# Making the top-k masks inside the first attention head pair, and filling that pair twice as densely

## The chip, the cores and the metric

The kernel runs on one core of a Trainium2 chip. The metric is the device time of one execution in microseconds. Times shown are of three runs of the kernel before; the rows are of one profiled execution.

## The reference

A two-layer streaming trunk on 1024 prompt positions and 64 sample positions (with 512 cached ones), all in one call. What matters here is the attention branch of layer 0:

```
rel   = relu(einsum('bqhd,bsd->bqhs', qi, ki))
score = einsum('bqh,bqhs->bqs', wi, rel)              # one score row per query
adm   = (kpos // 64) <= (qpos // 64)
top_val, top_idx = top_k(where(adm, score, -inf), k)  # 256 keys for a prompt row, 144 for a sample row
logits = einsum(q, k[top_idx]) * 64 ** -0.5
o      = softmax(logits) @ v[top_idx]                 # 8 heads, 2 key/value groups
a_out  = o * silu(ga)
```

The kernel gathers nothing. For each row it finds the k-th largest score by a search, and adds a mask (0 or -1e30) to the logits of all keys; equal scores at the threshold are taken in order of position until k is reached. Beside the attention, a gated short convolution and the projections of both layers have to be computed.

## The kernel before, in words

All activations lie transposed, 128 channels by 1088 positions (1024 prompt, 64 sample). A projection tile is 128 output channels; it is three chunks of positions, each 24 accumulated matmuls (8 slices of the contraction, three products of a high and a low part), 72 matmuls in all.

The layer 0 part goes in this order. The indexer's scores of the seven score blocks (six prompt blocks of 128 queries, whose key ranges are 384 to 1024 wide, and the sample's, 576 wide) are put side by side in one tile S of 4800 columns. `topk` (line 487) then searches the threshold T of every row by halving; its passes run on VectorE and ScalarE, while TensorE works at projection tiles. After that, `mask` (line 592) makes a row block's mask: a sign pass on ScalarE (line 601), and on VectorE a count (602), a comparison for equality (603), a running sum over the equal ones in the tile `cum` (604), and three more passes (605 to 607) that leave the mask in the bf16 tile `bias`. All seven are called in one loop (line 877), at the end of the pool of the search.

Then comes the attention, in four head pairs t = 0 to 3 (line 934). A pair makes its query stacks (`pair_stack`, on ScalarE and POOL), goes through the eight query blocks in the order ORDER[t] (0 to 7 in the first pair), and ends with the sample's. In `attend` a block b with n = 128 (b + 1) keys does, for each of its two heads, `softmax`: logits by TensorE in pieces of at most 512 columns, a fused add of the mask with a running minimum on VectorE into S (line 622), the exponential on ScalarE (625), a reciprocal on VectorE (626) and the scaling on POOL (627). Blocks 0 and 1 read a fixed corner tile in place of `bias`. `weighted` transposes the probabilities in groups of two key tiles on TensorE (650), splits them on ScalarE and VectorE (276, 277), and multiplies with the values (658). The two halves are added into q on VectorE (722; 732 for the sample, which closes the pair).

The probabilities are kept in S itself: `slot` hands out columns one after another and starts again at 0 at the end, so block 0 uses the columns 0 to 256, block 1 those to 768, and so on. S holds the scores until the masks have read them.

What the TensorE queue does between attention steps is laid down by hand. After the Q, K, V, convolution and gate tiles done so far, eleven projection tiles are left (ATTN_TILES): three for Q, four GB and four GA. Their matmuls are handed out one by one by a generator, `tiles` (line 919). First 255 are issued ahead of the pairs (BEFORE). Then each call of `pace` draws a number of them: RATE[t] = (r0, r1, r2) is drawn r0 at each logit piece, r1 at the end of each value group, r2 behind each full group of transposes. The generator takes the tiles in order, and a GA tile t is held until head pair t is done:

```python
while kind == GA and self.done <= t:
    yield
```

A step that meets this line issues nothing. What is left after the fourth pair is issued at once (line 945). The order on each engine's queue is then put together by a planner that takes the earliest traced instruction that its own estimate of durations says is ready; `issue_after` adds an edge that keeps an instruction behind a given one on the same engine. Loads all go through SyncE's queue.

Of the kernel before, what the change touches and what calls it, by code (L numbers as in the profile page):

```python
# [2 lines left out]

# [6 lines left out]
F32 = mybir.dt.float32  # L10
F32R = mybir.dt.float32r
BF = mybir.dt.bfloat16
I32 = mybir.dt.int32
AF = mybir.ActivationFunctionType
OP = mybir.AluOpType
PSUM = bass.MemoryType.PSUM

P = 128
D = 1024
KT = D // P  # L20
SEQ = 1024
DEC = 64
PAST = 512
TC = SEQ + 64
# [7 lines left out]
MASK = -1.0e30  # L32
# [40 lines left out]
NSB = len(SBLK)  # L73
# [11 lines left out]
ORDER = [(0, 1, 2, 3, 4, 5, 6, 7)] + [(7, 0, 6, 1, 5, 2, 4, 3)] * 3  # L85


BEFORE = 255
RATE = ((1, 1, 3),) * 4


def cut(n):
# [5 lines left out]
class Trunk:  # L98
# [388 lines left out]
    def topk(self, pool):  # L487
# [4 lines left out]
        V = nc.vector  # L492

        def t(name, w=NSB):
            return pool.tile([P, w], F32, name=name)

        kk = [TOPK_P] * (NSB - 1) + [TOPK_S]
        steps, upper = 23, 7
        self.kneg = kneg = t("kneg")
        lims, lad = t("lims", 4 * NSB).rearrange("p (i j) -> p i j", i=4), t("lad", steps)  # L500
        for j in range(NSB):
            n, k, p = SW[j], kk[j], slice(COL[j], COL[j] + 1)
# [5 lines left out]
            nc.gpsimd.memset(lad[:, s:s + 1], 2.0 ** -(s + 1))  # L508
        tiny = t("tiny")
        nc.gpsimd.memset(tiny, 2.0 ** -126)  # L510
        cv, m, sgn, limx, T, cand, flag = (t(n) for n in ("cv", "m", "sgn", "limx", "T", "cand", "flag"))
        self.T, self.cv, self.sgn = T, cv, sgn
        junks = [self.cum, pool.tile([P, SEQ], BF, name="junk")]


        small = self.bank("av", "small")
# [43 lines left out]
        for i in range(len(exps) + steps):  # L560
            for n, p in enumerate(SPANS):
                count(n, i < len(exps) + upper)
                if i < len(exps):
                    f, nxt = exps[i], (*exps, 1.0)[i + 1]
                    V.tensor_scalar(g[:, p], m[:, p], nxt - nxt / f, nxt / f, op0=OP.mult, op1=OP.add)
                    V.tensor_mul(cand[:, p], cand[:, p], g[:, p])
                    if i == len(exps) - 1:
# [8 lines left out]
                                       op0=OP.add, op1=OP.mult)  # L576
# [12 lines left out]
        V.tensor_mul(T, T, flag)  # L589
        V.tensor_mul(T, T, sgn)  # L590

    def mask(self, pool, j):

        V = self.nc.vector
        n = SW[j]
        sl = self.S[:, SOFF[j]:SOFF[j] + n]
        bi = self.bias[:, SOFF[j]:SOFF[j] + n]
        p = slice(COL[j], COL[j] + 1)
        thr, c = self.T[:, p], self.cv[:, p]
        cum = self.cum[:, 0:n]  # L600
        self.nc.scalar.activation(sl, sl, AF.Copy, scale=self.sgn[:, p])
        V.tensor_scalar(bi, sl, thr, self.kneg[:, p], op0=OP.is_gt, op1=OP.add, accum_out=c)
        V.tensor_scalar(bi, sl, thr, None, op0=OP.is_equal)
        V.tensor_tensor_scan(cum, self.ones.to_broadcast([P, n]), bi, c, OP.mult, OP.add)  # L604
        V.scalar_tensor_tensor(bi, cum, 0.0, bi, op0=OP.is_gt, op1=OP.mult)
        V.scalar_tensor_tensor(bi, sl, thr, bi, op0=OP.is_lt, op1=OP.add)
        V.tensor_scalar(bi, bi, MASK, None, op0=OP.mult)


    def softmax(self, slot, lhs, keys, g, n, bias):  # L610
# [151 lines left out]
    def layer0(self):  # L762
# [4 lines left out]
        def cols(c):  # L767
            return slice(*CHUNKS[c])

        def into(dst, f=AF.Copy):  # L770
            def evac(c, ps):
                nc.scalar.activation(dst[:, cols(c)], ps, f)
            return evac

        def into_z(z):
            def evac(c, ps):
                a, b = CHUNKS[c]
                for d, e in ((a, min(b, SEQ)), (SEQ, b)):
                    if d < e:
                        o = 2 if d < SEQ else 4  # L780
                        nc.scalar.activation(z[:, o + d:o + e], ps[:, d - a:e - a], AF.Copy)
            return evac
# [16 lines left out]
        def do(kind, t, evac):  # L799
            w = take(kind, t)  # L800
            fetch()
            return self.project(w, evac)

        with ExitStack() as es:
# [37 lines left out]
            kv = es.enter_context(self.pool("kv", "right"))  # L842
            self.kp = [kv.tile([P, 2, TC], F32R, name=f"kp{i}") for i in range(2)]
            self.vs = kv.tile([P, 13, 2, P], F32R, name="vs")
            with self.pool("search", "right") as se:
                def pair():
                    return (se.tile([P, TC], F32, tag="gc", name="gc"),
                            se.tile([P, TC + 4], F32, tag="z", name="z"))

                self.cum = se.tile([P, SEQ], BF, name="cum")  # L850
                self.topk(se)
                se.tile([P, 512], F32, tag="tap", name="place", bufs=1)
                kt, vt = pair()
                self.wslots.append((se, 2))
                hist = se.tile([P, 4, 2], F32, name="hist")
                self.load(hist, self.i["hist"])
                self.hist = hist
                self.tail = se.tile([P, 4, 2, 2], F32, name="tail")

                self.tags = ["pj", "pj", "lg", "lg", "lg"]  # L860
                do(Q_, 0, into(self.q[:, 0, :]))
                do(K_, 0, into(kt))
                do(V_, 0, into(vt))
                self.load(self.o["k"], kt)
                self.load(self.o["v"], vt[:, 0:TC])
                self.keys_values(se, kt, vt)
                for c in range(4):
                    if c >= NGZ:
                        do(GZ, c, into(self.bo[:, c, :], AF.Silu))
                    gc, z = pair()  # L870
                    do(GC, c, into(gc))
                    do(XIN, c, into_z(z))
                    self.conv(se, c, gc, z)
                self.wslots.remove((se, 2))
                self.tags = ["pj"]
                self.load(self.o["conv"], self.tail)
                for j in range(NSB):
                    self.mask(se, j)
            with self.pool("attn", "right") as ap:
                self.at = 0  # L880

                ap.tile([P, TC], F32, tag="ga", name="place")
                self.kc = [ap.tile([P, 2, NS], F32R, name=f"kc{i}") for i in range(2)]
                ap.tile([P, 256], F32, tag="ckr", name="place", bufs=1)
                ap.tile([64, 256], F32, tag="avl", name="place", bufs=2)
                ap.tile([P, P], F32R, tag="qs", name="place", bufs=1)
                ap.tile([P, 512], F32R, tag="ptl", name="place", bufs=2)
                ap.tile([P, 512], F32R, tag="pth", name="place", bufs=2)
                for e in range(2):
                    ap.tile([P, TC], F32R, tag=f"qst{e}", name="place")  # L890

                def gate_b(t):
                    def evac(c, ps):
                        nc.vector.tensor_mul(self.bo[:, t, cols(c)], self.bo[:, t, cols(c)], ps)
                    return evac

                ga = []

                def gate_a(t):
                    def evac(c, ps):  # L900
                        if c == 0:
                            ga[:] = [ap.tile([P, TC], F32, tag="ga", name="ga")]
                        g, q = ga[0], self.q[:, t, :]
                        if t == 3:
                            nc.scalar.activation(g[:, cols(c)], ps, AF.Silu)
                            nc.vector.tensor_mul(q[:, cols(c)], q[:, cols(c)], g[:, cols(c)])
                            return

                        nc.scalar.activation(g[:, cols(c)], ps, AF.Copy)
                        if c == NCH - 1:  # L910
                            nc.scalar.activation(g, g, AF.Silu)
                            nc.gpsimd.tensor_mul(q, q, g)
                    return evac

                evacs = {Q_: lambda t: into(self.q[:, t, :]), GB: gate_b, GA: gate_a}
                left = list(ATTN_TILES)
                self.done = 0

                def tiles():
                    while left:  # L920
                        kind, t = left[0]
                        while kind == GA and self.done <= t:
                            yield
                        key, w = ahead.pop(0)
                        assert key == (kind, t)
                        fetch()
                        yield from self.steps(w, evacs[kind](t), n=1)
                        left.pop(0)
                        yield

                self.side = tiles()
                for _ in range(BEFORE):
                    next(self.side)
                for t in range(4):
                    while (Q_, t) in left:
                        next(self.side)
                    self.rate = RATE[t]
                    st = self.pair_stack(ap, t)
                    for b in ORDER[t]:
                        self.attend(ap, st, t, b)  # L940
                    if t == 0:
                        self.sample_keys(ap)
                    self.attend_sample(ap, st, t)
                    self.done = t + 1
                for _ in self.side:
                    pass
                fetch()
# [273 lines left out]
```

## Time and profile before

| what | us |
|---|---|
| median of 3 runs | 1160.54 |
| lowest, highest | 1160.08, 1160.92 |
| the profiled execution's own time | 1162.17 |
| its span | 1160.5 |
| TensorE busy (share of the span) | 1087.5 (94%) |
| VectorE busy | 670.2 (58%) |
| ScalarE busy | 519.3 (45%) |
| POOL busy | 440.1 (38%) |

The span runs from the first to the last instruction of the program; the execution's own time has what lies around it. Busy times are sums over stages with different limits. In the rows PE is TensorE, DVE is VectorE, ACT is ScalarE, POOL is GpSimd, and L604 is line 604.

### The profile page before, as it was taken

The page shows a single profiled execution, that of the slowest core. Times are in us where ns is not written, and L with a number is a line of the kernel's source. Part 1 is how long each engine was busy: PE and PEld are TensorE (multiplying, and loading weights), DVE is VectorE, ACT ScalarE, POOL GpSimd, SP SyncE. Part 2 cuts the span into 40 slices and gives each one's busy share as a digit, 9 for nine tenths or more (in the row PEclk, how much of TensorE's full clock was granted, in tenths as well). Part 3 has the DMA queues.
Part 4 walks back from the last instruction along what each step waited for, and adds up shares of the span by engine and source line. Part 5 has one row for each costly group of instructions (what it writes and reads, how often), then busy time and mean ns, then how long its engine had stood idle before and what let it go on. Part 6 is the DMA issues. An engine that isn't in the chain of part 4 may idle for free.

```text
span 1160.5 us, 18892 instructions
## 1 busy us (share of the span) xinstructions
PE 1087.5 (94%) x7255; PEld 1044.7 (90%) x7255; DVE 670.2 (58%) x1657; ACT 519.3 (45%) x976; POOL 440.1 (38%) x454
## 2 busy tenths in 40 slices
PE   5899999999999449999999899999999999999997
PEld 4789689999999439989899899999999999999996
DVE  4711799998886987767675524521186055247134
ACT  5232586856777246777666313521121211135111
POOL 2634223466548225464431326531143111154222
PEclk9999999999999769999999999999999999999999
DMA  9745511211101000000002410111112111131012
GB/s 361 302 155 191 201 29 55 80 52 38 37 19 54 25 14 19 19 19 20 19 20 82 160 59 31 44 55 37 37 47 91 37 37 36 38 108 38 1 65 91
DMA packets 26074, 81.84 MB, mean 71 GB/s; under 512 B 3072, under 2 KB 9984, under 8 KB 23552
## 3 DMA queue, kind: packets, MB, share of 16 engines
q1 hardware_dynamic: 25984, 80.63, 19.7%
q8 instruction: 57, 0.93, 0.3%
q14 instruction: 33, 0.27, 0.1%
HBM read 74.50 MB, written 6.12 MB: 69 GB/s over the span
## 4 chain that ended last, share of the span: by engine, by line
PE 81%; DVE 7%; ACT 5%; POOL 3%; issue 3%; DMA 1%; SPq 0%; POOLq 0%; DVEq 0%; ACTq 0%
PE pj L247 40%; PE op L247 15%; PE pj L262 9%; PE av L658 3%; PE logit_ps L620 2%; PE p_ps L650 2%; PE ada_ps L153 2%; PE sgu_ps L1036 1%; PE score_ps L427 1%; PE first L318 1%; POOL w_lo L239 1%; POOL hf L329 1%; DVE cum L604 1%; PE score_ps L428 1%; DVE al L277 1%
## 5 line engine op out<-in xcount | busy, mean ns | idle before, releaser
L247 PE MATMUL pj<-ah,w_hi 128*128 128x364 f32 (+1 forms) x984 | 326.0, 331 | 1.0 <-ACT w_hi L238 1.0
L247 PE MATMUL pj<-al,w_hi 128*128 128x364 f32 (+1 forms) x984 | 323.8, 329 | 0.0
L247 PE MATMUL pj<-ah,w_lo 128*128 128x364 f32 (+1 forms) x984 | 323.1, 329 | 0.0
L239 POOL TENSOR_TENSOR w_lo<-w_raw,w_hi 128x1024 fp32r<-128x1024 f32 x63 | 158.0, 2510 | 341.3 <-ACT w_hi L238 336.4
L247 PEld LDWEIGHTS pj<-ah,w_hi 128*128 128x128 f32 x984 | 185.0, 188 | 2.0 <-ACT w_hi L238 1.3
L247 PEld LDWEIGHTS pj<-ah,w_lo 128*128 128x128 f32 x984 | 184.8, 188 | 0.3 <-issue 0.2
L247 PEld LDWEIGHTS pj<-al,w_hi 128*128 128x128 f32 x984 | 185.0, 188 | 0.0
L247 PE MATMUL op<-ah,w_lo 128*128 128x448 f32 (+2 forms) x384 | 126.2, 330 | 3.1 <-POOL w_lo L239 3.1
L247 PE MATMUL op<-al,w_hi 128*128 128x448 f32 (+2 forms) x384 | 126.5, 330 | 0.7 <-DVE al L277 0.6
L247 PE MATMUL op<-ah,w_hi 128*128 128x448 f32 (+2 forms) x384 | 126.9, 330 | 0.0
L238 ACT ACTIVATE w_hi<-w_raw 128x1024 fp32r<-128x1024 f32 x69 | 72.9, 1058 | 111.6 <-PE pj L247 83.2
L528 DVE TENSOR_SCALAR_CACHE_REDUCE cum<-S,cand 128x512 bf16<-128x512 f32 (+5 forms) x142 | 119.0, 838 | 2.0
L262 PE MATMUL pj<-ah,w_hi 128*128 128x364 f32 (+1 forms) x288 | 96.0, 334 | 0.0
L262 PE MATMUL pj<-ah,w_lo 128*128 128x364 f32 (+1 forms) x288 | 95.2, 330 | 0.0
L262 PE MATMUL pj<-al,w_hi 128*128 128x364 f32 (+1 forms) x288 | 95.1, 330 | 0.0
L976 DVE SCALAR_TENSOR_TENSOR x<-op,mod,x 128x192 f32<-128x192 f32 (+2 forms) x64 | 30.5, 497 | 108.2 <-PE op L247 108.2
L555 ACT ACTIVATE junk<-S,cand 128x896 bf16<-128x896 f32 (+2 forms) x78 | 77.7, 996 | 24.4 <-DVE m L558 20.6
L627 POOL TENSOR_SCALAR S<-S,sm 128x384 f32<-128x384 f32 (+8 forms) x68 | 50.8, 753 | 87.1 <-DVE sm L626 72.7
L620 PE MATMUL logit_ps<-kp,qst 128*128 128x384 f32 (+5 forms) x192 | 49.6, 366 | 33.2 <-DVE sm L622 32.6
L247 PEld LDWEIGHTS op<-ah,w_lo 128*128 128x128 f32 x384 | 73.1, 190 | 5.4 <-POOL w_lo L239 3.5
L247 PEld LDWEIGHTS op<-al,w_hi 128*128 128x128 f32 x384 | 73.0, 190 | 3.4 <-DVE al L277 1.4
L247 PEld LDWEIGHTS op<-ah,w_hi 128*128 128x128 f32 x384 | 73.0, 190 | 2.0
(242 smaller groups left out, 1973.9 us busy)
## 6 DMA issues: line engine op xcount, KB each, us to landing
w_raw<-in_w SPq DMA_DIRECT2D x53, 512.0 KB, 3.4
ada<-in_ada_w SPq DMA_DIRECT2D x19, 1024.0 KB, 7.8
w_raw<-in_wo SPq DMA_DIRECT2D x16, 512.0 KB, 3.4
x<-in_x SPq DMA_DIRECT2D x8, 544.0 KB, 6.5
bo<-in_ada_w SPq DMA_DIRECT2D x4, 1024.0 KB, 6.9
x<-in_x SPq DMA_DIRECT2D x1, 1792.0 KB, 10.2
out_y<-x SPq DMA_DIRECT2D x1, 1792.0 KB, 6.6
x<-in_x SPq DMA_DIRECT2D x1, 1536.0 KB, 8.2
```

Source lines behind the costliest of these rows:

```text
L153: nc.tensor.matmul(pt[32 * g:32 * g + 32, 0:P], self.cs[:, kt, :], raw(kt)[:, g * P:(g + 1) * P], start=kt == 0, stop=kt == KT - 1, tile_p ...
L238: nc.scalar.activation(hi, raw, AF.Copy)
L239: (nc.gpsimd if lo_eng == "pool" else nc.vector).tensor_sub(lo, raw, hi)
L247: last = self.nc.tensor.matmul(ps, wt[:, kt, :], at[:, kt, c0:c1], start=n == 0, stop=n == len(mms) - 1)
L262: self.nc.tensor.matmul(ps, wt[:, kt, :], at[:, kt, a:b], start=kt == 0 and i == 0, stop=kt == KT - 1 and i == 2)
L528: V.tensor_scalar(junks[0][:, 0:SW[j]], self.S[:, span(j)], thr, 0.0, op0=OP.is_lt, op1=OP.add, accum_out=col(cv, j))
L555: nc.scalar.activation(junks[1][:, 0:SW[j]], self.S[:, span(j)], AF.Sign, scale=-1.0, bias=col(cand, j), accum_out=col(cv, j))
L620: mm = nc.tensor.matmul(pt[:, 0:w], lhs, keys[i][:, g, s], start=i == 0, stop=i == 1)
L627: nc.gpsimd.tensor_scalar(p, p, st[:, 3:4], 0.0, op0=OP.mult, op1=OP.add)
L650: mm = nc.tensor.transpose(pt[0:r, o:o + P], p[:, j * P:j * P + r], self.ident)
L658: mm = nc.tensor.matmul(av[:, 0:m], self.vs[0:r, vbase + j, g, :], t[0:r, o:o + m], start=j == 0 and i == 0, stop=j == nj - 1 and i == 1)
L976: nc.vector.scalar_tensor_tensor(x[:, t, a:b], ps[:, a:b], self.mod[l][:, 16 + t, j:j + 1], x[:, t, a:b], op0=OP.mult, op1=OP.add)
```

## The change

The loop of seven masks ahead of the attention is gone. In the first pair, ahead of block b, the masks of MASKS[b] are made: masks 0, 1 and 2 before blocks 0, 1 and 2, masks 3 and 4 before block 3, mask 5 before block 4, mask 6 (the sample's) before block 5. Mask j serves block j + 2. Each mask's VectorE instructions are kept behind the last one of the mask before. The pool of the search is closed by then, so the four small tiles that masks need (T, cv, sgn, kneg) move to a pool that stays, and `cum` takes the place of the gate tile `ga` in the pool of the attention; the search gets a second scratch tile of its own. RATE becomes (2, 2, 6) in the first pair and (1, 1, 1) in the others.

```diff
+MASKS = ((0,), (1,), (2,), (3, 4), (5,), (6,), (), ())
+
+
 BEFORE = 255
-RATE = ((1, 1, 3),) * 4
+RATE = ((2, 2, 6), (1, 1, 1), (1, 1, 1), (1, 1, 1))
...
-        self.kneg = kneg = t("kneg")
+
+        cv, sgn, T, kneg = (self.keep.tile([P, NSB], F32, name=n) for n in ("cv", "sgn", "T", "kneg"))
+        self.T, self.cv, self.sgn, self.kneg = T, cv, sgn, kneg
...
-        cv, m, sgn, limx, T, cand, flag = (t(n) for n in ("cv", "m", "sgn", "limx", "T", "cand", "flag"))
-        self.T, self.cv, self.sgn = T, cv, sgn
-        junks = [self.cum, pool.tile([P, SEQ], BF, name="junk")]
+        m, limx, cand, flag = (t(n) for n in ("m", "limx", "cand", "flag"))
+        junks = [pool.tile([P, SEQ], BF, name=f"junk{i}") for i in range(2)]
...
-    def mask(self, pool, j):
+    def mask(self, j):
...
-        V.tensor_scalar(bi, bi, MASK, None, op0=OP.mult)
+        self.masked = V.tensor_scalar(bi, bi, MASK, None, op0=OP.mult).ins
...
+            self.keep = kv
             with self.pool("search", "right") as se:
...
-                self.cum = se.tile([P, SEQ], BF, name="cum")
                 self.topk(se)
...
-                for j in range(NSB):
-                    self.mask(se, j)
             with self.pool("attn", "right") as ap:
                 self.at = 0
 
-                ap.tile([P, TC], F32, tag="ga", name="place")
+                self.cum = ap.tile([P, 2 * TC], BF, tag="ga", name="cum")
...
                     for b in ORDER[t]:
+                        for j in MASKS[b] if t == 0 else ():
+
+                            with self.tc.issue_after(self.masked) if j else nullcontext():
+                                self.mask(j)
                         self.attend(ap, st, t, b)
```

## Rows read from the trace of the kernel before

**Rows 1.** The page, part 2: busy tenths in 40 slices of 29 us.
```profile
PE   5899999999999449999999899999999999999997
...
DVE  4711799998886987767675524521186055247134
...
PEclk9999999999999769999999999999999999999999
```

**Rows 2.** TensorE's waits, 380 to 640 us: total, times, longest.
```profile
PE logit_ps L620 <- DVE sm L622: 32.6, 4, 29.9
PE p_ps L650 <- DVE ptl L277: 2.0, 3, 1.0
PE av L658 <- ACT pth L276: 1.2, 1, 1.2
```

**Rows 3.** Timeline of TensorE around its stop: start, duration, instruction, idle before it.
```profile
390.05 0.40 PE L620 MATMUL logit_ps<-kp,qst 128*128 128x256 f32 x2
420.35 0.80 PE L620 MATMUL logit_ps<-kp,qst 128*128 128x256 f32 x2 [29.91 <-DVE sm L622]
```

**Rows 4.** VectorE's groups by line, 381.4 to 420.3 us: busy us, mean ns.
```profile
L604 DVE TENSOR_TENSOR_SCAN cum<-ones,cv,bias 128x384 bf16<-128x384 f32 (+6 forms) x7 | 11.5, 1638 | 0.0
L603 DVE TENSOR_SCALAR bias<-S,T 128x384 bf16<-128x384 f32 (+6 forms) x7 | 6.9, 1043 | 0.0
L606 DVE SCALAR_TENSOR_TENSOR bias<-S,T,bias 128x384 bf16<-128x384 f32 (+6 forms) x7 | 6.5, 932 | 0.2
L602 DVE TENSOR_SCALAR_CACHE_REDUCE bias<-S,T,kneg 128x384 bf16<-128x384 f32 (+6 forms) x7 | 6.4, 984 | 0.1
L605 DVE SCALAR_TENSOR_TENSOR bias<-cum,bias 128x384 bf16<-128x384 bf16 (+6 forms) x7 | 6.1, 865 | 0.0
L607 DVE TENSOR_SCALAR bias<-bias 128x384 bf16<-128x384 bf16 (+6 forms) x7 | 2.2, 316 | 0.0
```

**Rows 5.** The chain that ended last, where it passes into the masks: start, us.
```profile
369.98 11.46 PE pj L262 x69
381.44 3.33 DVE bias L602 x9
```

**Rows 6.** Line 732, the sample's output: two a pair; first and last start.
```profile
L732 DVE TENSOR_TENSOR q<-av,avl x8: 206/217/218, 479.9 to 622.1; 64x64 f32<-64x64 f32 x8
```

**Rows 7.** Busy us of PE, PEld, DVE, ACT, POOL; clock, DMA: pair 0, pairs 1-3.
```profile
420.40:480.30 59.90, 56.27 (x357) 51.56 (x358) 44.89 (x151) 42.97 (x96) 31.59 (x35) 0.94 0.06 17
480.30:622.40 142.10, 137.80 (x947) 130.96 (x946) 97.12 (x303) 97.31 (x204) 57.40 (x57) 1.00 0.06 20
```

**Rows 8.** Line 603 by forms; POOL's timeline beside it; line 1029 (min/median/max ns).
```profile
L603 DVE TENSOR_SCALAR bias<-S,T 128x768 bf16<-128x768 f32 x1 | 1.8, 1750 | 0.0
L603 DVE TENSOR_SCALAR bias<-S,T 128x512 bf16<-128x512 f32 x1 | 1.5, 1516 | 0.0
L603 DVE TENSOR_SCALAR bias<-S,T 128x1024 bf16<-128x1024 f32 x1 | 0.7, 741 | 0.0
...
386.48 6.04 POOL L699 TENSOR_TENSOR qst<-q,qst 64x512 fp32r<-64x512 f32 x4
...
L1029 DVE TENSOR_TENSOR vtok<-vtok,lnb x9: 1164/1205/2159, 854.2 to 888.8; 128x1024 f32<-128x1024 f32 x8, 64x1024 f32<-64x1024 f32 x1
```

**Rows 9.** Busy us as in rows 7: around the stop, and a later stretch.
```profile
395.00:420.00 25.00, 0.00 (x0) 0.00 (x0) 24.69 (x29) 0.14 (x1) 0.00 (x0) 0.50 0.00 0
...
424.00:428.00 4.00, 3.96 (x13) 3.30 (x13) 3.69 (x19) 3.60 (x12) 2.46 (x6) 0.50 0.00 0
...
640.00:660.00 20.00, 16.90 (x76) 15.52 (x76) 10.07 (x11) 6.09 (x9) 5.66 (x3) 0.91 0.32 106
```

**Rows 10.** Line 601, the sign pass: min/median/max ns, first and last start.
```profile
L601 ACT ACTIVATE S<-S,sgn x7: 617/822/1138, 367.4 to 380.3; 128x512 f32<-128x512 f32 x1, 128x640 f32<-128x640 f32 x1, 128x768 f32<-128x768 f32 x1, 128x576 f32<-128x576 f32 x1
```

**Rows 11.** VectorE's waits, 420.4 to 622.4 us: total, times, longest.
```profile
DVE ptl L277 <- ACT pth L276: 17.3, 33, 2.7
DVE sm L626 <- ACT S L625: 12.3, 24, 2.4
```

More of the change, by code (lines that the diff above doesn't have):

```diff
@@ L1 @@
-from contextlib import ExitStack, contextmanager
+from contextlib import ExitStack, contextmanager, nullcontext
 from itertools import chain
```

## The prediction

> **What bounds the kernel now.** I began with the page's 40 slices. TensorE is busy in nearly all of them; the one place where it stands is the two slices from 377 to 435 us, and there VectorE is at its fullest and the TensorE clock falls [rows 1]. Next came the waits of TensorE around that place: of 32.6 us waited on VectorE's running minimum in the logits, one wait is 29.9 us [rows 2]. The timeline says when: the last logits are issued at 390.05 and the next at 420.35 [rows 3]. What VectorE does meanwhile is in the groups of its lines: six operations for each of seven mask rows and nothing else of weight, 39.6 us together (11.5 + 6.9 + 6.5 + 6.4 + 6.1 + 2.2) [rows 4]. The chain of waits runs from the projection matmuls into the first mask operation at 381.44 [rows 5]. So: between the top-k search and the attention lies a stretch that belongs to VectorE alone, and TensorE has run out of projection work 30 us before it ends.
>
> The next question is what stands behind that gap, because work moved out of it lands there. The four sample outputs mark the ends of the head pairs: the first at 479.9, the last at 622.1 [rows 6], so the later pairs take (622.1 - 479.9)/3 = 47.4 us each, and pair 0 takes 59.9 us from 420.4. In pair 0 VectorE is busy 44.9 of 59.9 us (75%), in the later three 97.1 of 142.1 (68%), while TensorE is busy 94% and 97% [rows 7]. TensorE bounds the pairs, and VectorE has room in them, but in pair 0 only 15 us: the masks need some 40.
>
> **The filling, counted.** A pair calls for filling at 26 logit pieces, 22 value groups and 21 full transpose groups (eight blocks and the sample). At (1, 1, 3) that is 26 + 22 + 63 = 111 steps, at (2, 2, 6) 222, at (1, 1, 1) 69. But of the tiles left after the 255 steps, only GB0's remaining 33 matmuls and GB1's 72 can go in pair 0: the next tile, the gate GA0, is held until pair 0 is done, and a step that meets it issues nothing. So both kernels issue the same 105 matmuls in pair 0; the doubling only brings them earlier (96 in blocks 0 to 4, the rest in block 5), and blocks 6, 7 and the sample get none. After pair 0 both kernels have the same 432 left. The old pairs pace 333 of them, the new ones 207. A fill matmul costs 11.46/69 = 0.166 us [rows 5], so the 42 fewer per pair are worth 7.0 us a pair, and they come back as 3 x 7.0 = 21 us of matmuls behind the last pair. This part is worth nothing in sum as long as TensorE stays the bound: pairs of 47.4 - 7.0 = 40.4 us, at which VectorE's 97.1/3 = 32.4 us are 80%. That is the condition that the forecast rests on.
>
> **Removed.** The wait of 29.9 us [rows 2]. Nothing in blocks 0 and 1 needs a mask (they read the corner tile), so their logits may be reduced as soon as mask 0 no longer reads the S columns into which block 0 writes.
>
> **Given back in pair 0.** VectorE now does, from 381.44 on, the masks and pair 0 one among the other. Each block's probabilities go to S columns that masks read: block 1 stands behind mask 1, block 3 behind masks 3 and 4, block 5 behind mask 6. So all masks come before block 5, none can be put off, and what queues behind a mask on VectorE is the block's reduction, for which ScalarE's exponential, and the logits that want its PSUM bank, wait in turn. The VectorE work up to the first sample output:
> - masks: 39.6 us as measured, and 0.5 us because the seven counting passes follow no longer on each other and cost their full mean (7 x 0.984 = 6.9 for 6.4) [rows 4].
> - POOL: three of the seven comparisons at line 603 took 1.5 to 1.75 us while POOL made the query stacks, though the widest, later, took 0.74 [rows 8]: about 1.1 us each, already in the 39.6. In pair 0 POOL is busy 31.6/59.9 = 53% [rows 7], so I expect four of seven to be hit: 0.9 us more. Bounds: none hit (-3.3), all hit (+4.4). I take 41.0 in all.
> - pair 0: 44.9 us [rows 7], some of which is already pair 1's; it stands the same in both kernels.
>
> Together 85.9 us. VectorE was 99% busy with masks alone (24.69 of 25.00 us) [rows 9] and 75% in pair 0; masks fill the holes until block 5, so I take 96%: 89.5 us, and the first sample output falls at 470.9 instead of 479.9. Bounds: no contention and no hole, 381.4 + 81.7 = 463.1 (16.8 us gained); no overlap at all, 381.4 + 45 + 59.9 = 486.3 (6.4 us lost). TensorE's part of pair 0, some 56 us busy [rows 7], fits between 390.45 and 470.9.
>
> **At nothing.** The seven sign passes of ScalarE (line 601) run at 367 to 380 us, inside the search [rows 10], and depend on the same inputs as before; were they moved into pair 0, ScalarE's 43.0 of 59.9 us would cover the 5.8 (7 x 0.82). The larger scan tile takes the gate's place and is free before GA0 comes. The four small tiles, the second junk tile and the ordering edges issue no instruction. No DMA is added or moved past a queue: weight loads follow the tiles in the same order, and the 225 matmuls behind the last pair run at 72 to a tile, 12 us, a spacing like that of the fill before 390. The half-rate clock after the gap (0.50 at 424 to 428) goes too, in a stretch that is VectorE's now.
>
> **The sum.** -29.9 + 20.9 (what pair 0 takes longer, from 390) = -9.0 us, and 0 for the moved filling. The profiled execution took 1162.17 us around a span of 1160.5; it would come to 1153.2. It is 1.6 us above the median of the three runs, 1160.54, from which the forecast is **1151.5 us**.
>
> **Rivals.**
> *The pairs do not shorten (slower).* TensorE waits in pairs 1 to 3 where the filling was taken out: two matmuls fewer between the transposes and the products that need ScalarE's and VectorE's split of them. Already VectorE waits 17.3 us there for ScalarE, and 12.3 for the exponentials [rows 11]. If a pair stays at 47.4 us, the 21 us behind the last pair are a pure addition: 1151.5 + 21 = 1172.5. It decides from 3.0 us a pair on, that is at pairs over 43.4 us. Against it: at the transposes and the value products TensorE waits little now (2.0 and 1.2 us in all) [rows 2], and VectorE would be at 80%. Chance 0.16.
>
> *POOL in the way of every mask operation.* Lines 604 to 606, 21 instructions, read two operands from SBUF. No row has them beside POOL; a two-operand line elsewhere shows one of nine at 2.16 us where the median is 1.21 [rows 8]. Were each held for half a POOL instruction (31.59/35 = 0.90 us) in 53% of cases, 21 x 0.53 x 0.45 = 5.0 us more on VectorE: 5.2 at 96%, so 1156.7. Chance 0.15. [...]
>
> *Nothing gained.* VectorE loses time to block chains as in the old pair 0: at 87% busy, T = 381.4 + 85.9/0.87 = 480.1 and the time stays at 1160.5. Chance 0.13.
>
> *The clock falls in pair 0.* TensorE has 56 us of work in 80 us and, from block 6 on, no filling. After its stop of 30 us the clock was 0.50, even at 424 to 428 when the engine was issuing again, and over 640 to 660, where it was busy 16.9 of 20 us, it was 0.91 [rows 9]. [...] Chance 0.06. [...]
>
> **How the numbers follow.** Forecast as told 0.50, POOL 0.15: faster by over 0.2% (2.3 us, about what a measurement of this kernel can tell from no change) 0.65. Nothing gained: 0.13. Pairs that do not shorten, and the clock: slower 0.22. The range goes from a full cover in pair 0 and some better packing (1143) up into the slower case, to pairs near 45.5 us (1167), leaving out 0.2. The faster cases' own range is 1143 to 1158.
>
> **What would show it.** Right: no TensorE wait over some 5 us between 390 and 425; first sample output near 471, VectorE over 93% busy from 381 to 440; line 262 silent from about block 5 to the end of pair 0; pairs near 40 to 41 us and a solid run of some 225 fill matmuls behind the last. Wrong: pairs over 43.4 us; the first sample output at 480 or later; TensorE waits on VectorE of several us before each of blocks 2 to 5; a clock under 1 after 400.

## The result, and the profile after

The changed kernel takes 1172.17 us (median of 4 runs, 1169.03 to 1173.12) against 1160.73 for the kernel before: a ratio of 1.0094, 95% interval 1.0075 to 1.0114. It is slower, by 11 us (1%), where 9 us faster was forecast. The profiled execution took 1172.18 us, 10.0 more than the one before, with a span of 1170.4.

The page's slices first, to be laid beside [rows 1].

```profile
PE   5899999999999769998999899999999999999997
...
DVE  4711799998887998687742514421177055246134
...
PEclk9999999999999879999999899999999999999998
```

The gap of TensorE at 377 to 435 us has gone from 4 tenths to 7 and 6; there is no longer one stop. The waits of TensorE from 380 to 640 us say what it became (compare [rows 2]):

```profile
PE logit_ps L624 <- DVE sm L626: 11.6, 9, 3.3
PE p_ps L654 <- POOL S L631: 6.6, 4, 2.6
PE av L662 <- DVE ptl L280: 3.5, 7, 1.7
```

One wait of 29.9 us turned into nine of at most 3.3 and some other short ones. That is what the change set out to do. Yet the pairs hardly come earlier. The outputs of blocks (line 726, first and last start) and of the sample (736), after and before:

```profile
L726 DVE TENSOR_TENSOR q<-av,avl x64: 259/283/286, 403.2 to 607.3; 64x128 f32<-64x128 f32 x64
L736 DVE TENSOR_TENSOR q<-av,avl x8: 204/218/219, 477.8 to 612.8; 64x64 f32<-64x64 f32 x8
```
```profile
L722 DVE TENSOR_TENSOR q<-av,avl x64: 265/283/285, 432.1 to 618.7; 64x128 f32<-64x128 f32 x64
```

The first block's output comes at 403.2 instead of 432.1, a lead of 28.9 us. The pair's last, the sample's, comes at 477.8 instead of 479.9 [rows 6]: all but 2.1 us of the lead is used up inside pair 0. Where, the busy times by stretch tell, cut where the last mask ends (442.5), at the first sample output and at the last (columns as in [rows 7]):

```profile
381.40:442.50 61.10, 43.51 (x218) 38.74 (x218) 59.01 (x116) 23.12 (x52) 28.17 (x21) 0.80 0.07 24
442.50:477.80 35.30, 31.00 (x192) 26.14 (x191) 27.72 (x87) 25.00 (x52) 19.55 (x19) 0.98 0.05 16
477.80:612.60 134.80, 127.60 (x844) 115.03 (x844) 95.19 (x302) 89.29 (x195) 49.94 (x54) 0.99 0.03 9
```

While masks are made VectorE is busy 59.0 of 61.1 us (97%): it sets the pace, and block after block stands in its queue behind the masks. Then pair 0 needs another 35.3 us, in which VectorE is busy 79%.

So pair 0 gains next to nothing, and what is lost is lost behind it. Restricted to the filling matmuls (PE column), pairs 1 to 3 and what follows them until the output projection, before and after:

```profile
479.90:622.30 142.40, 73.23 (x354) 56.97 (x355) 3.18 (x6) 3.79 (x8) 1.00 0.06 20
622.30:634.30 12.00, 12.00 (x73) 11.79 (x71) 0.00 (x0) 1.41 (x3) 1.00 0.54 193
```
```profile
477.80:613.00 135.20, 55.80 (x251) 40.56 (x252) 2.10 (x4) 2.37 (x5) 0.99 0.03 9
613.00:643.30 30.30, 29.68 (x178) 29.16 (x176) 1.06 (x2) 2.81 (x6) 1.00 0.33 113
```

With 103 filling matmuls fewer (251 for 354) the three pairs became 7.2 us shorter, and behind them 178 are left for 73, which takes 18.3 us more. So the sum at the start of the output projection is -2.1 - 7.2 + 18.3 = +9.0 us; some 1 us more is added in that projection, and the span ends 9.9 us later.

### The profile page after: what moved, and what is told of

It reads as the page before. It is cut to its first block, busy times and chain, and to the rows that moved or that the text cites. A ratio compares the mean times of both kernels' runs of the same rounds, so it can differ in the third digit from the quotient of the medians.

```text
span 1170.4 us, 18862 instructions
## 1 busy us (share of the span) xinstructions
PE 1106.2 (95%) x7255; PEld 1051.8 (90%) x7255; DVE 672.0 (57%) x1657; ACT 516.6 (44%) x974; POOL 448.2 (38%) x454
## 3 DMA queue, kind: packets, MB, share of 16 engines
q1 hardware_dynamic: 25984, 80.63, 19.6%
## 4 chain that ended last, share of the span: by engine, by line
PE 79%; DVE 8%; ACT 5%; issue 3%; POOL 3%; DMA 2%; POOLq 0%; SPq 0%; DVEq 0%; ACTq 0%
PE pj L250 40%; PE op L250 15%; PE pj L265 8%; PE av L662 3%; PE logit_ps L624 2%; PE p_ps L654 2%; PE ada_ps L156 2%; PE sgu_ps L1042 1%; PE score_ps L430 1%; PE first L321 1%; POOL w_lo L242 1%; DVE S L626 1%; DVE ptl L280 1%; ACT pth L279 1%; DMA x<-in_x 1%
## 5 line engine op out<-in xcount | busy, mean ns | idle before, releaser
L532 DVE TENSOR_SCALAR_CACHE_REDUCE junk<-S,cand 128x512 bf16<-128x512 f32 (+5 forms) x142 | 119.0, 838 | 2.0
L631 POOL TENSOR_SCALAR S<-S,sm 128x256 f32<-128x256 f32 (+8 forms) x68 | 57.5, 852 | 90.9 <-DVE sm L630 75.3
L990 POOL TENSOR_TENSOR acc<-acc,sq 128x448 f32<-128x448 f32 (+2 forms) x40 | 40.0, 999 | 91.6 <-ACT sq L988 90.9
```

The lines of the kernel that those rows point to most:

```text
L532: V.tensor_scalar(junks[0][:, 0:SW[j]], self.S[:, span(j)], thr, 0.0, op0=OP.is_lt, op1=OP.add, accum_out=col(cv, j))
L631: nc.gpsimd.tensor_scalar(p, p, st[:, 3:4], 0.0, op0=OP.mult, op1=OP.add)
L990: nc.gpsimd.tensor_add(acc, acc, sq)
```

## The experiments

Two theories stood at the start. **Theory 1**: the loss comes from the thinned filling of pairs 1 to 3, and the masks inside pair 0 are nearly neutral. **Rival**: the masks inside pair 0 cost it (contention, the lower clock), and the filling is harmless. Each ratio below is to runs of the kernel before taken beside the run, with its 95% interval.

### One part of the change at a time

Masks only:
```diff
-RATE = ((2, 2, 6), (1, 1, 1), (1, 1, 1), (1, 1, 1))
+RATE = ((1, 1, 3),) * 4
```


> Masks inside the first pair as in the change, but the filling (1, 1, 3) in all pairs as before. Theory 1 (the thinned filling of pairs 1 to 3 costs the time: in the changed kernel 165.3 us pass from the first sample output at 477.8 to the last fill matmul at 643.1, before it was 154.2): the later pairs return to about 47.4 us, the first sample output stays near 478 to 480, and the time is 1157 to 1161 us. Rival (the masks inside pair 0 cost it, through contention and the lower clock): the time stays at 1168 us or more.

Measured: 1160.52 us, ratio to the kernel before 0.9996 (0.9987 to 1.0005). Its sample outputs and its two parts of pair 0:

```profile
L736 DVE TENSOR_TENSOR q<-av,avl x8: 204/217/218, 480.0 to 621.5; 64x64 f32<-64x64 f32 x8
```
```profile
381.40:442.50 61.10, 37.78 (x172) 31.42 (x171) 57.91 (x113) 21.87 (x50) 30.14 (x21) 0.80 0.07 24
442.50:480.00 37.50, 36.92 (x241) 34.55 (x240) 27.63 (x90) 26.56 (x55) 19.63 (x19) 0.96 0.01 2
```

The first sample output is at 480.0, to a tenth where it was with the masks ahead of the pair. Removing a stop of TensorE of 29.9 us is worth nothing here.

Filling only, on the kernel before:
```diff
-RATE = ((1, 1, 3),) * 4
+RATE = ((2, 2, 6), (1, 1, 1), (1, 1, 1), (1, 1, 1))
```


> The kernel before with only the new filling, (2, 2, 6) in the first pair and (1, 1, 1) in the others; masks stay ahead of the attention. Theory 1: pairs 1 to 3 take about 45 us each, some 180 matmuls are left behind the last one, and the time is 1160.5 + 11 = 1169 to 1174 us. Rival (the masks cost it): 1159 to 1162 us.

Measured: 1176.19 us, ratio 1.0128 (1.0111 to 1.0146).

```profile
L732 DVE TENSOR_TENSOR q<-av,avl x8: 206/218/219, 481.5 to 616.6; 64x64 f32<-64x64 f32 x8
```
```profile
481.50:616.80 135.30, 56.02 (x251) 40.63 (x252) 2.11 (x4) 2.36 (x5) 0.99 0.03 9
616.80:647.10 30.30, 29.67 (x178) 29.08 (x176) 1.06 (x2) 2.81 (x6) 1.00 0.32 112
```

These are the changed kernel's rows again: 251 and 178 matmuls, 135.3 and 30.3 us. Theory 1 holds, the rival falls: the loss is the new filling's, all of it. The time lies 2 us above the expected range, some 4 us over the changed kernel, and the first sample output comes 3.7 us later than there (481.5 for 477.8): beside the new filling the masks inside pair 0 give back about 4 us.

The doubling kept in pair 0 alone:
```diff
-RATE = ((2, 2, 6), (1, 1, 1), (1, 1, 1), (1, 1, 1))
+RATE = ((2, 2, 6), (1, 1, 3), (1, 1, 3), (1, 1, 3))
```


> The changed kernel with (1, 1, 3) in pairs 1 to 3, (2, 2, 6) kept in the first. Theory 1: pairs at 47 us, 1156 to 1161 us, and within 2 us of masks-only, since both issue the same 105 matmuls in pair 0. Rival (the doubled filling in pair 0 is what costs): over 1165 us.

Measured: 1161.83 us, ratio 1.0006 (0.9994 to 1.0018); first sample output at 478.1, pairs of 47.6 us. The doubling in pair 0 changes nothing that can be measured, so within the filling it is pairs 1 to 3.

### Does a pair shorten when filling is taken out?

The kernel before with no filling in pairs 1 to 3:
```diff
-RATE = ((1, 1, 3),) * 4
+RATE = ((1, 1, 3), (0, 0, 0), (0, 0, 0), (0, 0, 0))
```


> The kernel before with no filling at all in pairs 1 to 3; 432 fill matmuls (71.7 us) are left behind the last pair. It measures how long a pair takes by itself. Theory A (a pair is a chain of waits between the engines that hardly shortens without filling; 42 matmuls fewer took 2.5 us off a pair and not 7.0): pairs of 40 to 43 us, 1190 to 1210 us. Rival B (TensorE's work sets the pace, thinning by 42 was unlucky in its order): pairs of 47.4 - 111 x 0.166 = 29 to VectorE's 32.4 us, and 1160 to 1175 us.

Measured: 1177.87 us in one run. It doesn't answer the question: without an edge that holds them, the planner drew the leftover matmuls ahead into the pairs, 267 of them into pair 1 alone, which took 70.7 us. So they were held:
```diff
-                for _ in self.side:
-                    pass
+                with self.tc.issue_after(self.lastmm):
+                    for _ in self.side:
+                        pass
```
(lastmm is the last value product issued.)

> The kernel before with no filling in pairs 1 to 3, and the 432 matmuls left over held behind the last value product of the last pair (in no-fill-later they were drawn ahead into the pairs). A clean measure of a pair by itself. Theory A (a chain of waits): 41 to 44 us a pair, and 432 x 0.166 = 71.7 us behind the last: 1195 to 1215 us. Rival B (TensorE's own work sets the pace): 29 to 35 us a pair, 1160 to 1180 us.

Measured: 1190.89 us in one run, below the range that theory A gave. Sample outputs, the pairs' busy times, and the filling alone behind them; then three waits, from 482 to 610 us:

```profile
L733 DVE TENSOR_TENSOR q<-av,avl x8: 206/217/219, 477.4 to 592.4; 64x64 f32<-64x64 f32 x8
```
```profile
477.40:592.10 114.70, 96.12 (x596) 75.63 (x595) 90.24 (x298) 82.28 (x186) 42.92 (x52) 0.99 0.02 6
...
592.00:663.80 71.80, 71.80 (x432) 71.57 (x431) 3.19 (x6) 5.15 (x11) 1.00 0.18 63
```
```profile
ACT pth L276 <- PE av L658: 12.7, 15, 2.2
...
DVE ptl L277 <- ACT pth L276: 7.8, 12, 1.3
...
PE p_ps L650 <- DVE ptl L277: 6.7, 10, 1.1
```

A pair by itself takes (592.4 - 477.4)/3 = 38.3 us, under the 41 of theory A and over the 35 of rival B. VectorE is then busy 79%, ScalarE 72%, TensorE 84% (its weight loads 66%): no engine is full, and the waits go round, ScalarE for TensorE, VectorE for ScalarE, TensorE for VectorE. The pair is a chain of hand-overs. With three points the price of filling can be read off. In the kernel before a pair holds 354/3 = 118 filling matmuls, 19.6 us at 0.166 us each, and takes 47.4: the filling adds 9.1 us, 0.46 us for each us of its own. In the changed kernel 251/3 = 84, 13.9 us, and 45.0: 6.7 added, 0.48 for each. **At these rates about half of the filling lies in holes of the pair and is free; behind the last pair all of it is paid.** Taking 17.1 us of filling out of three pairs (103 x 0.166) and paying it behind them loses half of it and more.

Nearly the same amount of filling (369 matmuls in the three pairs for 354), drawn elsewhere:
```diff
-RATE = ((1, 1, 3),) * 4
+RATE = ((1, 1, 3), (2, 2, 1), (2, 2, 1), (2, 2, 1))
```


> The kernel before with as much filling in pairs 1 to 3 (117 steps for 111) drawn elsewhere: (2, 2, 1), two at logit pieces and group ends and one behind the transposes. If the amount in a pair counts: pairs of 47 to 48 us and 1159 to 1163 us. If the place behind the transposes counts, where TensorE would wait for the split of them: pairs of 49 us and more, over 1166 us.

Measured: 1171.7 us, ratio 1.0083 (1.0068 to 1.0098).

```profile
L732 DVE TENSOR_TENSOR q<-av,avl x8: 205/216/219, 480.7 to 630.6; 64x64 f32<-64x64 f32 x8
```

Pairs of 50.0 us, 2.6 more than before, where the 5 matmuls more in each are 0.8 us. The place counts as well as the amount. My reading, not shown by a run of its own: matmuls behind a transpose group lie in the hole in which ScalarE and VectorE split the transposes, and drawn at the logits they delay what VectorE waits for. Its waits for TensorE at the running minimum are 13.1 us here from 480 to 650 us, and 6.6 in the kernel before. The changed kernel's (1, 1, 1) takes its filling out at just that place.

A second buffer for the value products, on the changed kernel:
```diff
-        av = self.bank("av", "av")
+        self.flip = not getattr(self, "flip", False)
+        av = self.bank("av" if self.flip else "lg", "av")
```


> The changed kernel with the value products of every other block accumulated in one of the three logit banks, so that a block's products need not wait until the block before has been read out of the single av bank. If that bank sets the pace of thinly filled pairs: 44.9 us a pair falls to 42 or less, 1160 to 1165 us. If not, or if the logits miss the bank as much: 44 us or more, 1168 to 1176 us.

Measured: 1214.7 us, ratio 1.0469 (1.0452 to 1.0487), far outside both ranges; TensorE waits 26.1 us for scaled probabilities (420 to 680 us), where the changed kernel's waited 6.6 (380 to 640):

```profile
PE p_ps L655 <- POOL S L631: 26.1, 18, 5.5
```

Taking a bank from the logits in this way costs far more than the value products win. Whether their single bank is what holds the chain stays open.

### What sets the length of pair 0

Two of the six mask passes left out, in the masks-only kernel:
```diff
-        V.tensor_tensor_scan(cum, self.ones.to_broadcast([P, n]), bi, c, OP.mult, OP.add)
-        V.scalar_tensor_tensor(bi, cum, 0.0, bi, op0=OP.is_gt, op1=OP.mult)
```


> The masks-only kernel with the running sum (line 608) and the pass that uses it (609) left out of each mask, so keys with a score equal to the threshold are all masked; 20.2 us of VectorE work less. If VectorE's work sets the length of pair 0's first part: masks end near 422 us and the first sample output comes near 460 instead of 480. If TensorE (half clock, filling) sets it: the first sample output stays above 470.

Measured: 1140.34 us in one run.

```profile
L734 DVE TENSOR_TENSOR q<-av,avl x8: 205/217/218, 458.4 to 599.8; 64x64 f32<-64x64 f32 x8
```
```profile
378.90:420.20 41.30, 32.46 (x172) 27.12 (x170) 39.87 (x95) 21.43 (x50) 22.43 (x20) 0.92 0.07 23
420.20:458.40 38.20, 36.66 (x240) 33.11 (x240) 29.03 (x93) 26.50 (x55) 20.40 (x20) 1.00 0.04 15
```

Keys whose score equals the threshold are then all masked. From the first mask to the first sample output it is 79.5 us instead of 98.6 (masks-only): 19.1 us less for 20.2 us of VectorE passes removed. The first part went from 61.1 to 41.3, the second stayed at 38. So VectorE's mask work counts in full inside pair 0, as it did ahead of it. One reservation: VectorE was busy only 16.6 us less over both parts (68.9 for 85.5), so what was left took 3.6 us longer, and the TensorE clock was higher (0.92 for 0.80 in the first part). A few of the 19.1 us may be the clock's.

More filling for pair 0, on the changed kernel:
```diff
-... (GB, 0), (GB, 1), (GA, 0), (GB, 2), (GA, 1), (GB, 3), (GA, 2), (GA, 3)]
+... (GB, 0), (GB, 1), (GB, 2), (GB, 3), (GA, 0), (GA, 1), (GA, 2), (GA, 3)]
```


> The changed kernel with the four GB tiles ahead of the four GA tiles, so that the doubled filling of pair 0 finds matmuls for all of its 222 steps instead of 105; 108 are left behind the last pair instead of 225. Theory 1 (pair 0 is bound by chains of waits once the masks are done, TensorE idles in it): the 117 matmuls, 19.4 us, go into the holes of pair 0, the first sample output comes at 478 to 485, and the time is 1153 to 1160 us. Rival (TensorE is full in pair 0 too, by its clock): pair 0 grows by the whole 19.4 us, first sample output at 495 or later, 1170 us or more.

Measured: 1166.59 us, ratio 1.0048 (1.0029 to 1.0066), between the two expected ranges. The rows of pair 0, cut where the masks end, and the sample outputs:

```profile
379.00:440.00 61.00, 43.28 (x219) 38.55 (x218) 58.95 (x116) 23.11 (x52) 28.33 (x21) 0.83 0.07 24
440.00:485.20 45.20, 45.20 (x302) 43.61 (x301) 28.74 (x90) 25.55 (x52) 21.96 (x20) 1.00 0.08 24
```
```profile
L736 DVE TENSOR_TENSOR q<-av,avl x8: 206/217/218, 485.2 to 623.0; 64x64 f32<-64x64 f32 x8
```

The part with the masks is as long as in the changed kernel and holds no more matmuls (219 for 218): the added ones all fall behind it. That part grows from 35.3 to 45.2 us with TensorE full: the added 19.4 us cost 9.9, again about half. What filling costs beside the masks is seen in the rows above: 218 matmuls in that part of the changed kernel and 172 in masks-only, 61.1 us in both. There it is free.

### Relief for VectorE, and a version that gains

The last mask pass on ScalarE, in the masks-only kernel:
```diff
-        V.scalar_tensor_tensor(bi, sl, thr, bi, op0=OP.is_lt, op1=OP.add)
-        self.masked = V.tensor_scalar(bi, bi, MASK, None, op0=OP.mult).ins
+        self.masked = V.scalar_tensor_tensor(bi, sl, thr, bi, op0=OP.is_lt, op1=OP.add).ins
+        self.nc.scalar.activation(bi, bi, AF.Copy, scale=MASK)
```


> The masks-only kernel with the last pass of each mask, the multiplication by -1e30 (line 611), as a copy with a scale on ScalarE, which is busy 22 of 61 us there; 3.9 us of VectorE work less. If VectorE sets the first part of pair 0: first sample output near 476, 1155 to 1158.5 us, faster than both kernels. If not, or if the extra hand-over to ScalarE costs as much: 1159 to 1162 us.

Measured: 1159.16 us, ratio 0.9979 (0.9970 to 0.9989): faster than both kernels, by about the least that can be told. From first mask to first sample output it is 96.9 us for 98.6. Less than half of the 3.9 us came through, and the time lies in the second of the expected ranges. The trace shows one reason: the five passes left take 42.9 us, in masks-only they took 40.9 of the 44.4 for six, so VectorE's mask work fell by 1.5 us only.

The scaling of pair 0's probabilities moved from POOL to ScalarE, in the masks-only kernel:
```diff
-        nc.gpsimd.tensor_scalar(p, p, st[:, 3:4], 0.0, op0=OP.mult, op1=OP.add)
+        if self.done == 0:
+            nc.scalar.activation(p, p, AF.Copy, scale=st[:, 3:4])
+        else:
+            nc.gpsimd.tensor_scalar(p, p, st[:, 3:4], 0.0, op0=OP.mult, op1=OP.add)
```


> The masks-only kernel with the scaling of the probabilities in pair 0 (line 631) on ScalarE instead of POOL, so that POOL reads SBUF far less while the masks are made. If POOL stands in the way of mask operations with two SBUF operands: the mask instructions' durations sum to 41.5 to 43 us instead of 44.9, and the first sample output comes 2 to 4 us earlier. If the longer durations have another cause (the in-turn order): the sum stays at 44.9 and the time within 2 us of 1160.5 or above.

Measured: 1162.73 us, ratio 1.0007 (0.9997 to 1.0018). The six groups of mask passes sum to 44.4 us as in masks-only, although POOL is busy half as long (15.2 us from 381.4 to 442.0, for 30.1 up to 442.5). So it is not the scaling that lengthens the masks.

Early filling with the pass on ScalarE:
```diff
+                        self.rate = (2, 2, 6) if t == 0 and b < 5 else RATE[t]
                         self.attend(ap, st, t, b)
```
(with RATE (1, 1, 3) throughout and the GB tiles first)

> The kernel with the mask's last pass on ScalarE, all GB tiles ahead of the GA tiles, and filling (2, 2, 6) in blocks 0 to 4 of the first pair alone, (1, 1, 3) from block 5 on and in all later pairs: 159 matmuls in pair 0 for 111, 72 left behind the last pair for 99. If TensorE has room while VectorE makes the masks and only there: the first sample output stays at 97 to 99 us behind the first mask instruction and the time is 1153 to 1157 us. If the added 48 matmuls delay pair 0 by their 8 us: 1158 to 1161 us.

Measured: 1159.14 us, ratio 0.9986 (0.9976 to 0.9995), above the 1153 to 1157 expected. The filling alone, in the two parts of pair 0, here and in masks-only:

```profile
379.60:438.30 58.70, 27.20 (x126) 24.02 (x125) 2.11 (x4) 0.47 (x1) 0.80 0.07 25
438.30:475.70 37.40, 18.08 (x87) 13.62 (x86) 2.07 (x4) 0.00 (x0) 1.00 0.05 16
```
```profile
381.40:442.50 61.10, 20.83 (x88) 16.67 (x86) 1.58 (x3) 0.47 (x1) 0.80 0.07 24
442.50:480.00 37.50, 15.97 (x73) 12.17 (x73) 1.57 (x3) 0.00 (x0) 0.96 0.01 2
```

The first sample output comes 96.1 us behind the first mask (96.9 without the early filling), with 213 matmuls on the way for 161: there the added ones are free, as expected. But none are then left behind the last pair. The planner drew the leftovers into it; that pair holds 154 and takes 65.2 us, and its last sample output, at 640.3, comes behind the first matmuls of the output projection. The time is that of the version without early filling; what the filling would be worth if the rest were held is not shown.

Both moves to ScalarE and the early filling (the edits of the last three runs together):

> Both together: mask's last pass and pair 0's scaling on ScalarE, and the early filling. If both theories hold: 1150 to 1156 us. If ScalarE becomes late for pair 0 with both: above the early-filling kernel.

Measured: 1159.76 us, ratio 0.9979 (0.9969 to 0.9988), no better than the last pass on ScalarE alone, and outside the expected range.

## Why the prediction was wrong, point by point

**What bounds the kernel** was half right. The stop of 29.9 us and its cause were read correctly. "TensorE bounds the pairs" was not, as far as pairs 1 to 3 go: the 97% busy in [rows 7] came from filling put into the holes of a chain of hand-overs. Without it a pair takes 38.3 us at 84%, and the rows of busy time can't tell the two apart, since filling makes TensorE busy in any case.

**The counting of the filling** was right for pair 0: from 381.4 us to the first sample output both kernels issue about as many (161 and 158 in the traces), and the changed one only five after 451 us. It was off behind it. The three pairs hold 251 where 207 were counted, and 178 stand behind the last where 225 were to come (before: 354 for 333). So some 34 a pair were taken out and not 42.

**"This part is worth nothing in sum as long as TensorE stays the bound"** is the step that failed, and it makes the larger part of the error. It priced filling in a pair at its own length, 7.0 us for 42 matmuls; pairs of 40.4 us were to come. The pairs took 45.0: of the 5.7 us of the 34 matmuls 2.4 came back. The filling in a pair costs 0.46 to 0.48 of its length, so 7.2 us came back of the 18.3 paid behind: +11.1 instead of 0. The rival "the pairs do not shorten" named this mechanism, its place and its threshold of 43.4 us; I gave it 0.16. That its time of 1172.5 is what was measured is luck: it had pairs of 47.4 us, 21 us lost on them and 9 gained in pair 0, where 11.1 were lost and 2.1 gained. The rows for it stood in [rows 11], VectorE waiting for ScalarE; the same view has ScalarE waiting for VectorE, and [rows 7] has each of the two busy 68%:

```profile
ACT S L625 <- DVE sm L622: 15.0, 18, 2.2
```

**The first sample output** was forecast at 470.9 and came at 477.8. The VectorE work was sized well: 86.7 us (59.0 + 27.7) for 85.9. The masks took more, 44.5 us in the six groups where 41.0 were taken (39.6 before), the rest of the pair less. What failed is "I take 96%": VectorE reached 97% up to the last mask and 79% behind it, where no masks are left to fill its holes. 27.7 us at 96% would be 28.9; they took 35.3, and that is 6.4 of the 6.9 us. With the filling of before (masks-only) the same part took 37.5 us, and the gain was nil, with VectorE busy 87% (85.5 of 98.6 us): time and share as the rival "Nothing gained" had them, for that half of the change.

**Removed, 29.9 us**: the stop went, but it was never the price. What passed between the last filling ahead of the pairs and the first sample output was VectorE's masks and then the pair's chain, in either order: 98.5 us from the first mask on in the kernel before, 98.6 in masks-only. Short masks agree: 20.2 us of mask passes less, 19.1 us less to the first sample output.

**POOL in the way of mask operations** happened, at another place than I had priced it. Not the scaling in the pair (without it on POOL the sum stayed at 44.4), but a weight split and the making of pair 0's query stacks meet the first two masks. The timelines of VectorE and of POOL:

```profile
384.17 2.64 DVE L610 SCALAR_TENSOR_TENSOR bias<-S,T,bias 128x384 bf16<-128x384 f32 x1
386.85 1.23 DVE L611 TENSOR_SCALAR bias<-bias 128x384 bf16<-128x384 bf16 x1
...
389.68 2.32 DVE L608 TENSOR_TENSOR_SCAN cum<-ones,cv,bias 128x512 bf16<-128x512 f32 x1
392.04 1.71 DVE L609 SCALAR_TENSOR_TENSOR bias<-cum,bias 128x512 bf16<-128x512 bf16 x1
```
```profile
383.94 2.46 POOL L242 TENSOR_TENSOR w_lo<-w_raw,w_hi 128x1024 fp32r<-128x1024 f32 x1 [9.57 <-ACT w_hi L241]
386.48 6.71 POOL L703 TENSOR_TENSOR qst<-q,qst 64x512 fp32r<-64x512 f32 x4
```

Alone, in the kernel before, lines 610, 608 and 609 took 0.62, 1.28 and 0.68 us for the same widths. So 4.1 us are lost in three instructions beside POOL's weight split and stacks, where before the comparisons of line 603 lost 3.3 [rows 8]. Line 611, with one SBUF operand, lost another 1.0 (0.23 alone). That POOL is the cause is my reading of the overlap; no run took the stacks away.

**The clock** was 0.80 over the part with the masks (a mean of stretches at 0.50, as from 422 to 432 us, and at 1.00, as from 434 to 442), lower than I expected there. I gave its rival 0.06; no run shows what a lower clock costs. In that part VectorE sets the pace, busy 97%, and more filling there cost nothing (61.1 us with 218 matmuls in the changed kernel and with 172 in masks-only; with early filling 96.1 us to the first sample output, 96.9 without). The clock was 0.80 in all three. TensorE waited for VectorE seven times in that part of the changed kernel, up to 3.3 us; that these waits lower the clock was not shown. What a full clock would be worth there was not tried.

## What to carry to other kernels

A busy engine that is fed with filler is no proof that it is the bound: take the filler out once and measure the stage by itself, then price the filler by what it adds. Work that fills holes belongs where holes are; moved behind the stage it was paid in full here (432 matmuls behind the last pair took 71.8 us). Before a wait is removed, ask who makes the waiting engine wait: where that engine's work is only moved and not shortened, the end may not move, as in masks-only.

## What the runs showed of the hardware that I had not expected

Without any filling (the leftover held) the TensorE clock stayed at 0.99 over pairs 1 to 3, where its waits from 482 us on lasted 1.2 us at most. In pair 0 of the changed kernel, beside the masks, with waits of up to 3.3 us, it was 0.80. A running sum of 512 columns on VectorE took 2.32 us beside POOL's work in the changed kernel and 1.28 alone in the kernel before.
